# Down products of three feed-forward stages with act stationary and turned back to features

## The chip, the cores and the metric

The kernel runs on one core of a Trainium2 chip. The metric is the device time of one execution in microseconds (us). Five engines work side by side, each through its own queue of instructions: TensorE (PE, with weight loads as PEld), VectorE (DVE), ScalarE (ACT), GpSimd (POOL) and SyncE (SP, which here only issues transfers). They wait for one another by semaphores.

## The reference, cut to what matters

A trunk of two layers on 256 tokens with D = 1024 and a hidden width of 2816. Each layer is a half-weight feed-forward step, a mixer, and another half-weight feed-forward step:

```python
def swiglu(h, w_gate, w_up, w_down):
    return (jax.nn.silu(h @ w_gate) * (h @ w_up)) @ w_down
...
    h = x
    for layer in range(DEPTH):
        h = h + FFN_RESIDUAL_WEIGHT * swiglu(rmsnorm(h, ffn1_norm[layer]), ...)   # weight 0.5
        hn = rmsnorm(h, mix_norm[layer])
        if layer < N_A_LAYERS:
            h = h + mixer_a(hn, a_w_qkv[layer], a_w_o[layer], pos)
        else:
            h = h + mixer_b(hn, b_w_q[j], b_w_o[j], shared[0], shared[1], shared[2], pos)
        h = h + FFN_RESIDUAL_WEIGHT * swiglu(rmsnorm(h, ffn2_norm[layer]), ...)
        if layer == N_A_LAYERS - 1:
            shared = shared_kv(h, kv_norm, kv_w, pos)
    return rmsnorm(h, final_norm)
```

Everything is float32. The four feed-forward stages are called f10 (layer 0, first), f20 (layer 0, second), f11 and f21. They stand in the order f10, mixer a, f20, f11, mixer b, f21.

## The kernel before, in words

The residual lives in SBUF as hT: features on the 128 partitions (8 blocks), 256 tokens along the free axis. Norms work on it block by block: Norm.block(k) makes x_n, the block times its gain (ACT the high part, DVE the low part), and adds its square to a running sum ss_n (ACT squares, POOL adds). The column of scales (col_n, a small PE product at L236) is needed only later, as the products run on the unscaled x_n.

A float32 product is made of three products of a rounded type (fp32r): high by high, high by low and low by high. So each weight is split into a high part wh (ACT) and a low part wl (DVE), and so are the activations. There are two forms. With weights stationary (products_t), one matmul moves 512 columns (high and low of 256 tokens, L194) and one moves 256 (L197), and the result has features on the partitions. With activations stationary (product: L183, L185, L187) three matmuls move 512 columns of weights each, and the result has tokens on the partitions.

A feed-forward stage runs over the 22 blocks of 128 of the hidden width, two blocks at a time. ffn_blocks makes gate and up by products_t. close() evacuates a block's two results with joined() (L338: ACT copies one half out of PSUM and DVE adds the other), multiplies by the row of norm scales, takes Silu on ACT, multiplies, and splits the result into high and low: act. Blocks are closed one step behind the products.

The down product has two versions. For f10, f20 and f11, down_t (L319) runs over the eight blocks of features in pairs, each over all 22 hidden blocks, by products_t; when a pair of feature blocks is done, DVE adds both halves into hT (L331) and Norm.block starts the next norm. For f21, down_last (L434) has act stationary. It views the product of each pair of hidden blocks as a 2 by 2 by 2 product of quarters (two halves of tokens, two hidden blocks, two halves of features). Most pairs take eight products; the pairs in FAST (2, 4, 6 and 7) take seven, with sums of quarters on both sides. The sums of activations are made in the gate and up stage (quarter_sums), those of weights in load() by DVE and POOL (L466 to L468, named sum_f_d). The last two pairs (tail) are held, and the four quarters of the result are closed one after another over them. collect() spreads the shared products m1, m5, m6 and m7 over the four quarters.

PSUM has eight banks: five for accumulators (accp, tag acc) and three for turned tiles and others (trp, tag tr). In down_last c11, c12, c21, m1 and m5 are of accp, and c22, m6 and m7 of trp.

The mixers project q, k and v with x_n stationary and run the heads' work from an Agenda: a list of calls with due times in modelled PE microseconds, from which the next call is taken while the projections go on. A pair of heads passes scores, soften (ACT's exponential), scale (L617, by the sums' reciprocals), turn (PE transposes) and values (PE, L636 and L638). The last two pairs of heads have scale on DVE, the others on POOL. The plans written out at the mixer calls give the due times; ending() gives those of the last pairs.

Transfers go mostly through SP's queue in program order; rawp (4 buffers) and wp (8) set how far ahead they run. The opening loads the first gate and up pieces small, two gate pieces and the gains from ACT's queue and the rest, with xT, from SP's.

Of the kernel before, what the change touches and what calls it, by code (L numbers as in the profile page):

```python
# [35 lines left out]
         ("ffn1_norm", 1), ("mix_norm", 1), ("ffn2_norm", 1)]  # L36

# [26 lines left out]
def trunk(ctx: ExitStack, tc: tile.TileContext, a: dict, out: bass.AP):  # L64
# [141 lines left out]
    def by_token(xs):  # L206

        return [[tuple(x[:, i, t * P:(t + 1) * P] for i in range(2)) for x in xs] for t in range(NT)]

    class Norm:  # L210

        def __init__(self, gi, name):
            self.gi, self.name, self.x, self.col, self.row = gi, name, [], None, None
# [103 lines left out]
    def down_t(name, w, blocks, norm):  # L319

        for p in range(KD // 2):
            acs = [acc(f"dn_{name}_{2 * p + b}") for b in range(2)]
            for k0 in range(0, KF, KD):
                k = min(KD, KF - k0)
                ws = unit(f"{name}_{p}_{k0}", k, S, [(None, rows(w, k0, k, p * S, S))])
                cut = [[tuple(v[:, b * P:(b + 1) * P] for v in pair) for pair in ws] for b in range(2)]
                products_t(acs, cut, blocks[k0:k0 + k], k0 == 0, k0 + k == KF)
            for b, ac in enumerate(acs):
                d = 2 * p + b
                for half in (ac[:, :S], ac[:, S:]):  # L330
                    nc.vector.scalar_tensor_tensor(hT[:, d, :], half, 0.5, hT[:, d, :], op0=ALU.mult, op1=ALU.add)  # L331
                norm.block(d)

    def joined(ac, name):

        s = etile(f"j_{name}")
# [524 lines left out]
```

## Time and profile before

| what | value |
|---|---|
| median of 3 runs | 988.2 us (987.77 to 988.45) |
| the profiled execution | 988.49 us, span 986.7 us |
| mean granted TensorE clock | 0.998 |
| busy, share of the span | PE 99%, PEld 86%, DVE 77%, ACT 60%, POOL 20% |
| f10's down (old form) | about 133.1 to 194.3 us |
| f20's down (old form) | about 435.0 to 496.2 us |
| f11's down (old form) | about 619.9 to 681.1 us |
| f21's down (act stationary) | about 923.2 to 980.4 us, then the last norm and the output |

The span runs from the first to the last instruction, and the execution's time has some 1.8 us more around it. A row of the timeline gives start, duration, engine, line, operation, the tile written and those read, and in brackets the idle time before it and what released it. Matmuls are pipelined: what a matmul costs is the time from its start to the next start, not its duration. A row of the windows gives the stretch and its length, then busy time and instructions for PE, PEld, DVE, ACT and POOL, the granted clock, DMA share and GB/s.

### The profile page before, as it was taken

How to read it: one execution, taken by the hardware profiler on the slowest of the kernel's cores; microseconds unless marked ns; L12 is line 12 of the kernel's file. 1: busy time of each engine (PE TensorE's matmuls, PEld its weight loads, DVE VectorE, ACT ScalarE, POOL GpSimd, SP SyncE). 2: the span in 40 equal slices, each digit the busy share in tenths (PEclk: the TensorE clock that was granted, in tenths of full speed). 3: DMA queues.
4: the chain of work that ended last, by engine and by line, in shares of the span. 5: the costliest groups of instructions: out<-in, count | busy, mean ns of one | idle time of the engine just before them, and what ended most of it. 6: DMA issues, size and time to landing. Idle time of an engine off the chain costs nothing.

```text
span 986.7 us, 15270 instructions
## 1 busy us (share of the span) xinstructions
PE 974.5 (99%) x5640; PEld 847.9 (86%) x5640; DVE 755.7 (77%) x1329; ACT 594.3 (60%) x1090; POOL 200.5 (20%) x204
## 2 busy tenths in 40 slices
PE   8999999999999999999999999999999999999997
PEld 5888888888889888888888888888888988888886
DVE  5987866677888788876668887657677878888996
ACT  7656654457776565655546656644577766666562
POOL 3211111122302211110112111011042122112461
PEclk9999999999999999999999999999999999999999
DMA  9786565654433566556655565665544255565341
GB/s 303 244 261 199 175 204 191 213 171 163 134 107 124 171 200 191 184 193 201 201 183 171 176 208 175 201 193 200 191 132 147 90 168 160 183 198 186 129 171 43
DMA packets 152395, 176.03 MB, mean 178 GB/s; under 512 B 3584, under 2 KB 140288, under 8 KB 152320
## 3 DMA queue, kind: packets, MB, share of 16 engines
q1 hardware_dynamic: 151600, 174.24, 55.0%
q8 instruction: 44, 0.72, 0.3%
q10 hardware_dynamic: 720, 0.82, 0.2%
q14 instruction: 31, 0.25, 0.1%
HBM read 173.99 MB, written 1.05 MB: 177 GB/s over the span
## 4 chain that ended last, share of the span: by engine, by line
PE 68%; DVE 2%; ACT 2%; issue 1%; POOL 0%; POOLq 0%; ACTq 0%; DVEq 0%
PE f_g L194 12%; PE f_u L194 12%; PE dn_f L194 8%; PE f_u L197 6%; PE f_g L197 6%; PE dn_f L197 4%; PE dn_f_d L187 1%; PE dn_f_d L185 1%; PE dn_f_d L183 1%; PE q_b L183 1%; PE kv_b L183 1%; PE q_b L187 1%; PE q_b L185 1%; PE kv_b L187 1%; PE kv_b L185 1%
## 5 line engine op out<-in xcount | busy, mean ns | idle before, releaser
L194 PE MATMUL f_g<-x_n,wh_f_g 128*128 128x512 f32 x688 | 180.5, 394 | 0.0
L194 PE MATMUL f_u<-x_n,wh_f_u 128*128 128x512 f32 x688 | 177.3, 390 | 0.0
L370 POOL TENSOR_TENSOR j_f_u<-j_f_u,r_n 128x256 f32<-128x256 f32 x88 | 81.9, 933 | 373.9 <-DVE j_f_u L338 351.5
L194 PEld LDWEIGHTS f_u<-x_n,wh_f_u 128*128 128x128 f32 x688 | 129.1, 188 | 27.3
L194 PEld LDWEIGHTS f_g<-x_n,wh_f_g 128*128 128x128 f32 x688 | 124.0, 189 | 22.8
L194 PE MATMUL dn_f<-act_f,wh_f 128*128 128x512 f32 x528 | 126.5, 391 | 0.0
L158 DVE TENSOR_TENSOR wl_f_u<-raw_f_u,wh_f_u 128x1024 fp32r<-128x1024 f32 x86 | 118.5, 1381 | 1.5 <-ACT wh_f_u L157 1.4
L194 PEld LDWEIGHTS dn_f<-act_f,wh_f 128*128 128x128 f32 x528 | 96.8, 188 | 18.6
L158 DVE TENSOR_TENSOR wl_f_g<-raw_f_g,wh_f_g 128x1024 fp32r<-128x1024 f32 x86 | 103.4, 1230 | 11.7 <-PE f_g L197 6.9
L158 DVE TENSOR_TENSOR wl_f<-raw_f,wh_f 128x1024 fp32r<-128x1024 f32 x72 | 81.8, 1153 | 35.5 <-ACT wh_f L157 26.7
L197 PE MATMUL f_u<-x_n,wl_f_u 128*128 128x256 f32 x688 | 103.3, 283 | 0.0
L197 PE MATMUL f_g<-x_n,wl_f_g 128*128 128x256 f32 x688 | 102.9, 282 | 0.0
L197 PEld LDWEIGHTS f_g<-x_n,wl_f_g 128*128 128x128 f32 x688 | 96.5, 190 | 6.3
L157 ACT ACTIVATE wh_f<-raw_f 128x1024 fp32r<-128x1024 f32 x72 | 67.3, 978 | 49.4 <-PE dn_f L194 27.1
L157 ACT ACTIVATE wh_f_g<-raw_f_g 128x1024 fp32r<-128x1024 f32 x86 | 89.4, 1048 | 11.3 <-issue 6.0
L157 ACT ACTIVATE wh_f_u<-raw_f_u 128x1024 fp32r<-128x1024 f32 x86 | 86.8, 1047 | 15.2 <-PE f_g L194 10.9
L197 PEld LDWEIGHTS f_u<-x_n,wl_f_u 128*128 128x128 f32 x688 | 91.6, 192 | 0.0
L231 POOL TENSOR_TENSOR ss_n<-ss_n,sq_n 128x256 f32<-128x256 f32 x42 | 41.3, 983 | 245.1 <-ACT sq_n L230 244.2
L368 ACT ACTIVATE j_f_g<-j_f_g 128x256 f32<-128x256 f32 x88 | 36.7, 417 | 68.9 <-DVE j_f_g L367 68.3
L95 ACT ACTIVATE act_f<-j_f_g 128x256 fp32r<-128x256 f32 x80 | 33.2, 417 | 66.2 <-DVE j_f_g L378 65.9
L197 PEld LDWEIGHTS dn_f<-act_f,wl_f 128*128 128x128 f32 x528 | 68.1, 191 | 2.8
L197 PE MATMUL dn_f<-act_f,wl_f 128*128 128x256 f32 x528 | 69.0, 283 | 0.0
(555 smaller groups left out, 1788.7 us busy)
## 6 DMA issues: line engine op xcount, KB each, us to landing
raw_f_g<-in_ffn_w_gate_dram SPq DMA_DIRECT2D x43, 1024.0 KB, 5.4
raw_f_u<-in_ffn_w_up_dram SPq DMA_DIRECT2D x43, 1024.0 KB, 5.4
raw_f<-in_ffn_w_down_dram SPq DMA_DIRECT2D x24, 1024.0 KB, 5.1
raw_f_d<-in_ffn_w_down_dram SPq DMA_DIRECT2D x11, 1024.0 KB, 5.0
raw_f<-in_ffn_w_down_dram SPq DMA_DIRECT2D x12, 768.0 KB, 4.6
raw_qka<-in_a_w_qkv_dram SPq DMA_DIRECT2D x16, 512.0 KB, 4.2
raw_va<-in_a_w_qkv_dram SPq DMA_DIRECT2D x4, 1024.0 KB, 5.2
raw_ao<-in_a_w_o_dram SPq DMA_DIRECT2D x4, 1024.0 KB, 5.0
```

Source lines behind the costliest of these rows:

```text
L95: nc.scalar.activation(hi, src, AF.Copy, scale=scale)
L157: nc.scalar.activation(wh, r, AF.Copy)
L158: nc.vector.tensor_sub(wl, r, wh.bitcast(F32))
L183: nc.tensor.matmul(ac, xh, wh, start=first, stop=False)
L185: nc.tensor.matmul(ac, xh, wl, start=False, stop=False)
L187: nc.tensor.matmul(ac, xl, wh, start=False, stop=last)
L194: nc.tensor.matmul(ac, wh, flat(x), start=first and i == 0, stop=False)
L197: nc.tensor.matmul(ac[:, :S], wl, x[:, 0, :], start=False, stop=last and i == len(ws) - 1)
L231: nc.gpsimd.tensor_tensor(self.ss, self.ss, sq, op=ALU.add)
L368: nc.scalar.activation(g, g, AF.Silu)
L370: nc.gpsimd.tensor_tensor(u, u, norm.row, op=ALU.mult)
```

## The change

down_t goes. The body of down_last becomes quartered(), which makes the four quarters and returns close(), and which both down() (f10, f20, f11) and down_last() (f21) call. down() takes 0.5 of the four quarters into SBUF tiles, turns each half of the features back with PE transposes, four to a tile of 512 columns, and DVE adds each tile into two blocks of hT. The first half of the features is turned within the last closing; the second half is put in norm.late and is turned after the first products of what follows: in ffn_blocks after the first hidden block's first feature, in the mixers from the Agenda at 1.5 and 2.0. f10 and f20 take seven products in four pairs, f11 in three, as the places that hold its sums are fewer there (homes). The order in which the accumulators are taken changes: m1, c11, c21, c12 and c22 are of accp, and m5, m6 and m7 of trp.

At the opening, gains and xT are one tensor, and the third gate piece goes to ACT's queue. In the mixers scale is on POOL for all pairs, and mixer a's plan has the turns of its last pairs later.

```diff
@@ -102,13 +105,11 @@
         return trp.tile([P, 512], F32, tag="tr", name=name)
 
 
-    hT = const.tile([P, KD, S], F32, name="hT")
-
-    gT = const.tile([P, len(GAINS) * KD], F32, name="gT")
-    nc.scalar.dma_start(gT, a["gains"])
-    early = [rawp.tile([P, 2, 1, S], F32, tag="raw", name=f"raw_0_{k}") for k in range(2)]
-    for k, raw in enumerate(early):
-        nc.scalar.dma_start(raw[:, 0, 0], a["ffn1_w_gate"][0][k * P:(k + 1) * P, :S])
+    both = const.tile([P, GX + KD * S], F32, name="gains_hT")
+    gT, hT = both[:, :GX], both[:, GX:].rearrange("p (k s) -> p k s", s=S)
+    early = {k: rawp.tile([P, 2, n, S], F32, tag="raw", name=f"raw_0_{k}") for k, n in OPENING[:3]}
+    for k, n in OPENING[:3]:
+        nc.scalar.dma_start(early[k][:, 0], a["ffn1_w_gate"][0][k * P:(k + n) * P, :S].rearrange("(k p) n -> p k n", p=P))
     BF16 = mybir.dt.bfloat16
     fill = const.tile([P, 512], BF16, name="fill")
     nc.vector.memset(fill, 1.0)
...
-        for k, n in ((0, 1), (1, 1), (2, 2), (4, 2), (6, 2)):
-            raw = early[k] if k < len(early) else rawp.tile([P, 2, n, S], F32, tag="raw", name=f"raw_0_{k}")
+        for k, n in OPENING:
+            raw = early.get(k) or rawp.tile([P, 2, n, S], F32, tag="raw", name=f"raw_0_{k}")
             wh, wl = [wp.tile([P, 2, n, S], F32R, tag=tag, name=f"{tag}_0_{k}") for tag in ("wh", "wl")]
             before(k, n)
-            for i, w in list(enumerate((wg, wu)))[k < len(early):]:
+            for i, w in list(enumerate((wg, wu)))[k in early:]:
                 nc.sync.dma_start(raw[:, i], rows(w, k, n, 0, S))
             nc.scalar.activation(wh, raw, AF.Copy)
...
@@ -315,21 +317,6 @@
             self.split(i + LEAD)
             return self.parts[i]
 
-
-    def down_t(name, w, blocks, norm):
-
-        for p in range(KD // 2):
-            acs = [acc(f"dn_{name}_{2 * p + b}") for b in range(2)]
-            for k0 in range(0, KF, KD):
-                k = min(KD, KF - k0)
-                ws = unit(f"{name}_{p}_{k0}", k, S, [(None, rows(w, k0, k, p * S, S))])
-                cut = [[tuple(v[:, b * P:(b + 1) * P] for v in pair) for pair in ws] for b in range(2)]
-                products_t(acs, cut, blocks[k0:k0 + k], k0 == 0, k0 + k == KF)
-            for b, ac in enumerate(acs):
-                d = 2 * p + b
-                for half in (ac[:, :S], ac[:, S:]):
-                    nc.vector.scalar_tensor_tensor(hT[:, d, :], half, 0.5, hT[:, d, :], op0=ALU.mult, op1=ALU.add)
-                norm.block(d)
 
     def joined(ac, name):
 
...
+                    while norm.late:
+                        norm.late.pop(0)()
                 if first is not None:
                     for k in range(KD - 2, KD):
...
@@ -423,21 +412,38 @@
         close_all()
         return blocks
 
-    def ffn(name, layer, which, norm, after, first=None, beside=()):
+    def left_sums(homes):
+
+        sums = {}
+        for i, home in zip(FAST, homes):
+            if home == "qkh":
+                parts = ap_.tile([P, 2, 512], F32R, tag=home, name=f"left_{i}", bufs=2)
+                sums[i] = (parts[:, 0], parts[:, 1])
+            elif home == "pT":
+                sums[i] = tuple(pp.tile([P, 512], F32R, tag=home, name=f"left_{i}_{j}") for j in range(2))
+            else:
+                sums[i] = tuple(xp.tile([P, 512], F32R, tag=f"{home[:2]}{int(home[2]) + j}", name=f"left_{i}_{j}")
+                                for j in range(2))
+        return sums
+
+    def ffn(name, layer, which, norm, after, first=None, beside=(), homes=("kx4", "kx6", "qkh", "qkh")):
         wg, wu, wd = (a[f"ffn{which}_w_{n}"][layer] for n in ("gate", "up", "down"))
-        blocks = ffn_blocks(name, wg, wu, norm, first, beside)
+        sums = left_sums(homes)
+        blocks = ffn_blocks(name, wg, wu, norm, first, beside, sums)
         if which == 1:
             table(AF.Exp, blocks[-1][:, 0, 0:1].bitcast(F32))
-        down_t(name, wd, blocks, after)
-
-
-    def down_last(name, w, blocks, sums, h, weight, part, after, tail=2):
-
-
-
-
-        c11, c12, c21, m1, m5 = [acc(f"dn_{name}_{n}") for n in ("11", "12", "21", "m1", "m5")]
-        c22, m6, m7 = [trt(f"dn_{name}_{n}") for n in ("22", "m6", "m7")]
+        down(f"{name}_d", wd, blocks, sums, after)
+
+
+    def quartered(name, w, acts, sums, weight, collected, tail=2):
+
+
+
+
+
+        blocks = [[tuple(x[:, i, t * P:(t + 1) * P] for i in range(2)) for x in acts] for t in range(NT)]
+        m1, c11, c21, c12, c22 = [acc(f"dn_{name}_{n}") for n in ("m1", "11", "21", "12", "22")]
+        m5, m6, m7 = [trt(f"dn_{name}_{n}") for n in ("m5", "m6", "m7")]
         begun = set()
 
         def add(n, ac, x, ws, last=False):
...
@@ -483,17 +489,13 @@
                 add(n, ac, left, right, last and len(n) == 1)
 
         def collect():
-
             a, b, c, d = [atile([P, 512], name=f"co_{name}_{n}") for n in "abcd"]
             nc.scalar.activation(a, m1, AF.Copy, scale=weight)
             nc.vector.scalar_tensor_tensor(b, m6, weight, a, op0=ALU.mult, op1=ALU.subtract)
-            nc.gpsimd.tensor_tensor(h[0][0], h[0][0], a, op=ALU.add)
             nc.vector.scalar_tensor_tensor(c, m7, weight, b, op0=ALU.mult, op1=ALU.subtract)
             nc.vector.scalar_tensor_tensor(b, m5, -weight, b, op0=ALU.mult, op1=ALU.add)
-            nc.gpsimd.tensor_tensor(h[0][1], h[0][1], b, op=ALU.add)
             nc.vector.scalar_tensor_tensor(d, m5, -weight, c, op0=ALU.mult, op1=ALU.subtract)
-            nc.vector.tensor_add(h[1][0], h[1][0], c)
-            nc.vector.tensor_add(h[1][1], h[1][1], d)
...
@@ -513,18 +515,63 @@
                             add(*quarters[t][c], blocks[t][2 * i + k], ws[2 * k + c])
             else:
                 held += [(2 * i + k, ws[2 * k:2 * k + 2]) for k in range(2)]
-        end = acc(f"dn_{name}_end")[:, :S]
+
+        def close(t, c, cols=slice(0, 512), ac=None, between=None):
+            n = quarters[t][c][0] if ac is None else "end"
+            whole = quarters[t][c][1] if ac is None else ac
+            to = whole[:, :cols.stop - cols.start]
+            for j, (k, ws) in enumerate(held):
+                add(n, to, blocks[t][k], tuple(v[:, cols] for v in ws[c]), k == KF - 1)
+                if between is not None and j == len(held) - 2:
+                    between()
+            return whole
+
+        return close
+
+    def down(name, w, acts, sums, norm):
+
+        outs = []
+        close = quartered(name, w, acts, sums, 0.5, outs.extend)
+
+        def turn(c, half):
+            tr = trt(f"dt_{name}_{c}_{half}")
+            for i in range(2):
+                for t in range(NT):
+                    at = i * S + t * P
+                    nc.tensor.transpose(tr[:, at:at + P], outs[t][c][:, (2 * half + i) * P:(2 * half + i + 1) * P], ident)
+            d = 4 * c + 2 * half
+            h = hT[:, d:d + 2, :]
+            nc.vector.tensor_add(h, tr.rearrange("p (k s) -> p k s", s=S), h)
+            for i in range(2):
+                norm.block(d + i)
+
+        def turn_first():
+            for half in range(2):
+                turn(0, half)
+
+        for c in range(2):
+            for t in range(NT):
+                ac = close(t, c, between=turn_first if (t, c) == (0, 1) else None)
+                nc.vector.scalar_tensor_tensor(outs[t][c], ac, 0.5, outs[t][c], op0=ALU.mult, op1=ALU.add)
+        norm.late += [lambda half=half: turn(1, half) for half in range(2)]
+
+    def down_last(name, w, acts, sums, h, weight, part, after):
+
+
+        def collected(shared):
+            for t in range(NT):
+                for c in range(2):
+                    (nc.vector if t else nc.gpsimd).tensor_tensor(h[t][c], h[t][c], shared[t][c], op=ALU.add)
+
+        close = quartered(name, w, acts, sums, weight, collected)
         for t in range(NT):
             for c in range(2):
-                n, ac = quarters[t][c]
-                cut = 512 if (t, c) != (1, 1) else S
-                for k, ws in held:
-                    add(n, ac[:, :cut], blocks[t][k], tuple(v[:, :cut] for v in ws[c]), k == KF - 1)
+                n = 512 if (t, c) != (1, 1) else S
...
@@ -603,18 +650,18 @@
                 for t, seg in enumerate(segs):
                     nc.vector.tensor_tensor_reduce(sm[:, seg], ps[i][:, seg], mask[:, seg], scale=-SCALE, scalar=3e38,
                                                    op0=ALU.add, op1=ALU.min, accum_out=nm[:, i, t:t + 1])
-                agenda.after(0.7 + 0.7 * i, soften, sm, nm[:, i], ls[:, i], p >= H // 2 - 2)
-
-        def soften(sm, nm, ls, last):
+                agenda.after(0.7 + 0.7 * i, soften, sm, nm[:, i], ls[:, i])
+
+        def soften(sm, nm, ls):
             for t, seg in enumerate(segs):
                 nc.scalar.activation(sm[:, seg], sm[:, seg], AF.Exp, bias=nm[:, t:t + 1], scale=-1.0,
                                      accum_out=ls[:, t:t + 1])
-            agenda.after(1.3, scale, sm, ls, nc.vector if last else nc.gpsimd)
-
-        def scale(sm, ls, engine):
+            agenda.after(1.3, scale, sm, ls)
+
+        def scale(sm, ls):
             nc.vector.reciprocal(ls, ls)
             for t, seg in enumerate(segs):
-                engine.tensor_scalar(sm[:, seg], sm[:, seg], ls[:, t:t + 1], None, op0=ALU.mult)
+                nc.gpsimd.tensor_scalar(sm[:, seg], sm[:, seg], ls[:, t:t + 1], None, op0=ALU.mult)
 
         def turn(p, i):
             tr = trt(f"pt_{name}{p}_{i}")[:, :3 * P]
...
         agenda = Agenda()
+        for norm in {id(norm): norm for norm, _, _ in segs}.values():
+            for i in range(len(norm.late)):
+                agenda.after(1.5 + 0.5 * i, lambda norm=norm: norm.late.pop(0)())
         scores, turn, values = attention(agenda, lambda g: (qks[g], vss.get(g)), mask, name, blocks)
 
...
           [steps(0, 3.0, 8.0, 11.0, 13.8, 16.5, 19.3), steps(1, 3.0, 8.0, 11.0, 13.8, 16.5, 19.3), steps(2, 4.0, 9.2),
-           steps(3, 2.4, 5.0) + ending(7.6)],
+           steps(3, 2.4, 5.4) + ending(8.4)],
           a["a_w_o"][0], masks[:, 0, :], n2)
     ffn("f20", 0, 2, n2, n3)
     kx = []
-    ffn("f11", 1, 1, n3, n5, beside=[lambda k=k: kx.append(gain(k, 3, "kx", "kx")) for k in range(KD)])
+    ffn("f11", 1, 1, n3, n5, homes=("qkh", "qkh", "pT"), beside=[lambda k=k: kx.append(gain(k, 3, "kx", "kx")) for k in range(KD)])
     xkv, xq = by_token(kx), n5.xs()
     wq, wkv = a["b_w_q"][0], a["kv_w"]
     kv = [(n3, xkv, [("k", wkv, g * n, n, g), ("v", wkv, H * DH + g * n, n, g)]) for g in range(2)]
```

More of the change, by code (lines that the diff above doesn't have):

```diff
@@ L206, in by_token @@
     def by_token(xs):
-        return [[tuple(x[:, i, t * P:(t + 1) * P] for i in range(2)) for x in xs] for t in range(NT)]
+        return [lambda k, t=t: tuple(xs[k][:, i, t * P:(t + 1) * P] for i in range(2)) for t in range(NT)]
     class Norm:
         def __init__(self, gi, name):
-            self.gi, self.name, self.x, self.col, self.row = gi, name, [], None, None
+            self.gi, self.name, self.x, self.late, self.col, self.row = gi, name, [], [], None, None
         def block(self, k):
@@ L523, in down_last @@
                 nc.vector.scalar_tensor_tensor(h[t][c], ac, weight, h[t][c], op0=ALU.mult, op1=ALU.add)
-                part(t, slice(c * 512, c * 512 + cut))
+                part(t, slice(c * 512, c * 512 + n))
             if t:
-                for k, ws in held:
-                    add("end", end, blocks[t][k], tuple(v[:, S:] for v in ws[1]), k == KF - 1)
+                end = close(1, 1, slice(S, 512), acc(f"dn_{name}_end")[:, :S])
                 hc = h[1][1][:, S:]
@@ L737, in first @@
     def first(k, n):
[L738 removed]
+        cols = slice(GX + k * S if k else 0, GX + (k + n) * S)
+        nc.sync.dma_start(both[:, cols], a["gains_xT"][:, cols])
         for i in range(k, k + n):
```

24 lines of the change are left out of this document (10 added, 14 removed).

## The prediction

> **What bounds the kernel now.** I read the page first (share of each engine, the slices, the groups), then the windows of the stages that change, then PE's timeline at the seams.
>
> ```profile
> span 986.7 us, 15270 instructions
> PE 974.5 (99%) x5640; PEld 847.9 (86%) x5640; DVE 755.7 (77%) x1329; ACT 594.3 (60%) x1090; POOL 200.5 (20%) x204
> PEclk9999999999999999999999999999999999999999
> ...
> L194 PE MATMUL dn_f<-act_f,wh_f 128*128 128x512 f32 x528 | 126.5, 391 | 0.0
> ...
> L197 PE MATMUL dn_f<-act_f,wl_f 128*128 128x256 f32 x528 | 69.0, 283 | 0.0
> ```
> ```profile
> core 0: us, PE busy (x) PEld busy (x) DVE busy (x) ACT busy (x) POOL busy (x), PEclk, DMA share, GB/s
> 133.10:194.30 61.20, 61.20 (x354) 54.06 (x353) 38.49 (x49) 29.78 (x42) 7.78 (x6) 1.00 0.62 201
> 923.20:981.00 57.80, 57.47 (x266) 47.88 (x264) 50.54 (x54) 28.61 (x42) 28.82 (x14) 1.00 0.29 101
> 800.00:923.00 123.00, 123.00 (x717) 108.76 (x716) 101.33 (x173) 75.20 (x140) 24.58 (x26) 1.00 0.59 188
> ```
>
> PE is busy 99% of the span and the granted clock stands at its top all the way, so the time is the sum of matmul slots plus a few microseconds in which PE waits. The first window is a down of the old form (f10's): gapless, 61.2 us. The second is f21's, which already has act stationary. The third is a gate and up stage that already makes quarter sums (f21's): PE 123.00 of 123 with DVE at 101.33. So fewer matmul slots become time one for one unless a wait takes their place. The profiled run took 988.49 us, of which the span is 986.7; the median shown is 988.2, 0.3 less. I sum against 988.49 and take 0.3 off. A change under 0.2% (2 us) cannot be told from none here.
>
> **The downs of f10, f20 and f11, slots.**
>
> ```profile
> 923.21 0.40 PE L183 MATMUL dn_f_d<-wh_f_d_0a,act_f 128*128 128x512 f32 x1
> 925.28 0.39 PE L183 MATMUL dn_f_d<-wh_f_d_0a,act_f 128*128 128x512 f32 x1
> ...
> 965.17 0.39 PE L187 MATMUL dn_f_d<-wh_f_d_8a,act_f 128*128 128x512 f32 x1
> ```
> ```profile
> 832.81 0.60 PE L789 MATMUL h<-ident,hT 128*128 128x128 f32 x4
> 833.16 2.09 PE L194 MATMUL f_g<-x_n,wh_f_g 128*128 128x512 f32 x8
> ...
> 844.39 0.60 PE L789 MATMUL h<-ident,hT 128*128 128x128 f32 x4
> ```
>
> Removed in each down: 176 matmuls of 512 and 176 of 256 columns (8 feature blocks by 22), 61.2 us by the first window. Added: an ordinary pair of blocks is 8 products of 3 matmuls, a fast one 7, so 7 x 24 + 4 x 21 = 252 matmuls of 512 for f10 and f20, and 8 x 24 + 3 x 21 = 255 for f11. The matmul at 965.17 starts 176 matmuls after that at 925.28, 39.89 us, hence 0.2266 us each; 252 are 57.1 us and 255 are 57.8 us. Turning back adds 16 transposes. The nearest rows are turn_h's: between its groups of four at 832.81 and 844.39 lie 32 pairs of (512, 256); at 61.2/176 = 0.3477 these take 11.13 of the 11.58 us, so four transposes cost 0.45 us and sixteen 1.8. Gain: 61.2 - 57.1 - 1.8 = 2.3 us for f10 and f20 each, 61.2 - 57.8 - 1.8 = 1.6 for f11; together **-6.2 us**.
>
> [...]
>
> **A bank that comes free late.** In quartered() the five accumulators of accp are now m1, c11, c21, c12, c22; before, c22 lay in a bank of trp. The pool's five banks pass on from the last gate and up results, and c22 gets that of the gate of block 21. c22 is begun by the tenth matmul of the down (three each for c11, c12, c21 first); in f21's down of before that is the row at 925.28. It now waits until DVE's joined() has added up that gate. Before, m1 had that bank, and m1 is not used until pair 2. The rows of f21's down start of before, DVE first and POOL below:
>
> ```profile
> 923.07 1.12 DVE L91 TENSOR_TENSOR act_f<-j_f_g,act_f 128x256 fp32r<-128x256 f32 x1 [0.48 <-ACT act_f L95]
> 924.12 2.32 DVE L454 TENSOR_TENSOR wl_f_d_2a<-raw_f_d,wh_f_d_2a 128x1024 fp32r<-128x1024 f32 x1
> 926.36 0.41 DVE L338 TENSOR_TENSOR j_f_g<-f_g,j_f_g 128x256 f32<-128x256 f32 x1
> ...
> 929.48 0.41 DVE L338 TENSOR_TENSOR j_f_u<-f_u,j_f_u 128x256 f32<-128x256 f32 x1
> ```
> ```profile
> 922.62 1.30 POOL L467 TENSOR_TENSOR sum_f_d_2b<-sum_f_d_2ac,raw_f_d 128x512 f32<-128x512 f32 x1 [0.49 <-PE f_u L197]
> 923.87 1.48 POOL L467 TENSOR_TENSOR sum_f_d_4b<-sum_f_d_4ac,raw_f_d 128x512 f32<-128x512 f32 x1
> 925.32 2.26 POOL L468 TENSOR_TENSOR sum_f_d_2d<-sum_f_d_2b,raw_f_d 128x512 f32<-128x512 f32 x1
> ```
> ```profile
> 133.21 0.42 DVE L338 TENSOR_TENSOR j_f_g<-f_g,j_f_g 128x256 f32<-128x256 f32 x1
> ```
>
> DVE works in order: act's low part, wl of pair 2, then the join, which ends at 926.36 + 0.41 = 926.77, where the tenth matmul is due at 925.28: PE stands 1.5 us, and all products behind it with it. The order of DVE's instructions at this place is the same in the four downs of the changed kernel, as POOL's sums now run in all four: 4 x 1.5 = **+6.0 us** (f21's down had no such wait before, so it pays without a gain). The ends: in f10 of before, where no sums ran, the join started 0.12 us after the down did (133.21 against 133.10) and would have cost nothing; if act's low part comes one POOL sum later, some 1.2 us more. So 0 to 2.7 each; I take the f21 row, as the changed stages are copies of that one. m1 now gets the bank of block 21's up result, free at 929.89, and m1 starts after 48 matmuls, 10.9 us into the down: no wait.
>
> The two DVE operations ahead of the join are stretched: 1.12 where the same work needs 0.4, and 2.32 where a lone 128x1024 one needs 1.22 (a row below). Each ends just as a POOL sum does. [...]
>
> **Mixer ends.**
>
> ```profile
> 276.97 0.55 DVE L617 TENSOR_SCALAR sm_a<-sm_a,ls_a 128x128 f32<-128x128 f32 x2
> 277.78 0.55 DVE L617 TENSOR_SCALAR sm_a<-sm_a,ls_a 128x128 f32<-128x128 f32 x2
> ...
> 280.77 0.56 DVE L617 TENSOR_SCALAR sm_a<-sm_a,ls_a 128x128 f32<-128x128 f32 x2
> 281.58 0.55 DVE L617 TENSOR_SCALAR sm_a<-sm_a,ls_a 128x128 f32<-128x128 f32 x2
> 282.33 1.22 DVE L310 TENSOR_TENSOR wl_ao<-raw_ao,wh_ao 128x1024 fp32r<-128x1024 f32 x1 [0.20 <-ACT wh_ao L308]
> ...
> 770.81 1.45 DVE L617 TENSOR_SCALAR sm_b<-sm_b,ls_b 128x128 f32<-128x128 f32 x6
> 772.36 0.55 DVE L617 TENSOR_SCALAR sm_b<-sm_b,ls_b 128x128 f32<-128x128 f32 x2
> ```
> ```profile
> 284.48 0.36 PE L636 MATMUL po_a<-pT_a,vs_a 128*128 128x256 f32 x1 [1.50 <-DVE vs_a L93]
> ...
> 774.57 0.39 PE L636 MATMUL po_b<-pT_b,vs_b 128*128 128x256 f32 x1 [1.02 <-DVE pT_b L91]
> ```
> ```profile
> 270.63 2.99 POOL L617 TENSOR_SCALAR sm_a<-sm_a,ls_a 128x128 f32<-128x128 f32 x4 [6.31 <-DVE ls_a L615]
> ```
>
> These two waits, 1.50 and 1.02, are PE's only ones of size between the opening and the end. Both end with DVE. DVE loses four times 0.55 = 2.2 us just ahead of the first and 2.0 ahead of the second, more than each wait. The scales go to POOL, 2.99/4 = 0.75 us each, in which a late pair's turn could be held; the plan of mixer a therefore moves its turns later (5.0 to 5.4, 7.6 to 8.4). Between -2.5 and +1 I take **-2.0**, nearer the end that the rows name.
>
> **Opening and seams.**
>
> ```profile
> 10.13 0.50 PE L194 MATMUL f_g<-x_n,wh 128*128 128x512 f32 x1 [0.62 <-ACT wh L172]
> ...
> 14.75 0.39 PE L197 MATMUL f_g<-x_n,wl 128*128 128x256 f32 x1 [0.47 <-DVE wl L173]
> ```
> ```profile
> 198.18 0.41 DVE L331 SCALAR_TENSOR_TENSOR hT<-dn_f,hT 128x256 f32<-128x256 f32 x1
> ```
> ```profile
> 199.59 0.74 POOL L231 TENSOR_TENSOR ss_n<-ss_n,sq_n 128x256 f32<-128x256 f32 x1 [1.61 <-ACT sq_n L230]
> ```
> ```profile
> 202.54 0.50 PE L236 MATMUL col_n<-mean,ss_n 128*128 128x1 f32 x4
> ```
>
> The opening loses one load (the gains join xT) and a gate piece goes from SP's queue to ACT's, where two early pieces stand ahead of it. The two waits shown, 1.1 us, are behind weight pieces: between -1.1 (both go) and +1.1 (the up piece lands later by as much) I take **-0.3**. At the seam to mixer a, features 4 to 7 used to arrive one by one, the last add at 198.18; now they come in two turns that start only after three products of the mixer. The last sum of squares ended at 200.33 and its column product starts at 202.54, 2.2 us of cover, of which I expect about all to go: **+0.3** (0 to 1.1). The seams to f11 and mixer b have the same late turns and no column product as near: nothing, and 0.5 each if their transposes come ahead of the closing addition.
>
> Sum: -6.2 + 6.0 - 2.0 - 0.3 + 0.3 = -2.2 us: 986.3 for a run like the profiled one, **986.0** against the median.
>
> **The rivals.**
>
> The bank comes free in time: DVE gets ahead of POOL, as in the 133.21 row. Then 986.0 - 6.0 = 980.0. For it speaks that half a microsecond earlier at 923.07 lets wl of pair 2 pass; against it that the very stage to be copied shows the contrary. It is also where I go if PE reaches the tenth matmul later than I think. Chance 0.20.
>
> Slower: DVE becomes the bound of the three downs. It is busy 38.49 of 61.2 us in f10's down; with the sums and the split of seven factors f21's took 50.54 of 57.8, and f10, f20 and f11 must also split the next stage's first weights and eight normed blocks. From 57.1 us of work on, PE waits for its low parts: at 59 to 60 us, 2.5 us in each down and 7.5 in all, 993.5. Against it: f21's PE was busy 57.47 of 57.80 with that load. Chance 0.25, with the deeper bank wait (2.7 us each, 990.8) in it, since it has the same cause.
>
> Mixer ends and opening bring nothing: POOL's four scales stand in a row of 3 us and hold the turn instead of DVE. 986.0 + 2.3 = 988.3. [...] Chance 0.12.
>
> **How the numbers follow.** The forecast gets 0.43; its own range is 984 to 988. The range runs from 979 (most of the first rival) to 993 (most of the second). Faster by over 0.2% (under 986.2): 0.23 of the forecast, all 0.20 of the first rival, 0.02 of the third: 0.45. Within 0.2%: 0.18 and 0.08, with 0.01 of the slower rival: 0.27. Slower by over 0.2% (above 990.2): 0.02, 0.24 and 0.02: 0.28.
>
> **What would show it.** Right: PE's groups show act-stationary downs at 0.2266 us a matmul, the tenth of each down with about 1.5 us idle put down to DVE's join of block 21's gate, and no idle before the po matmuls at the mixer ends. Wrong: no idle at the tenth matmul (first rival), idle spread over the downs and put down to DVE's wl (second), or the mixers' waits standing with POOL's scale as releaser (third).

## The result and the profile after

The changed kernel takes 1000.55 us (median of 4 runs, 999.73 to 1002.56) against 988.33 us for the kernel before on the same chip: a ratio of 1.0128, 95% interval 1.0116 to 1.0140. It is 1.3% slower, where 0.2% faster was forecast, and outside the range of 979 to 993. The profiled run took 999.77 us, its span is 998.0.

The page of after, its span, the engines and the chain of work that ended last:

```profile
span 998.0 us, 14866 instructions
PE 972.3 (97%) x5391; PEld 834.3 (84%) x5391; DVE 816.0 (82%) x1383; ACT 614.9 (62%) x1131; POOL 262.2 (26%) x242
...
PE 42%; DVE 16%; ACT 7%; issue 4%; POOL 3%; DMA 1%; POOLq 0%; ACTq 0%; DVEq 0%; SPq 0%
```

The same chain before:

```profile
PE 68%; DVE 2%; ACT 2%; issue 1%; POOL 0%; POOLq 0%; ACTq 0%; DVEq 0%
```

PE has less to do (972.3 us against 974.5) in a span that is 11.3 us longer, and the chain, 68% PE before, now runs through DVE, ACT and POOL as well. The stages, from the start of a stage's first matmul to that of the next, show where (the last column is the first experiment below):

| stage | before | after | old order of accumulators |
|---|---|---|---|
| opening, gate and up of f10 | 133.09 | 132.41 | 132.66 |
| down of f10 | 61.25 | 63.94 | 58.04 |
| mixer a | 117.14 | 119.67 | 119.65 |
| gate and up of f20 | 123.57 | 123.56 | 123.56 |
| down of f20 | 61.25 | 61.26 | 58.08 |
| gate and up of f11 | 123.57 | 124.41 | 124.41 |
| down of f11 | 61.25 | 64.51 | 58.75 |
| mixer b | 116.74 | 117.54 | 117.54 |
| gate and up of f21 | 125.35 | 125.33 | 125.33 |
| down of f21 to the end | 63.49 | 65.37 | 63.68 |

The downs, whose slots alone were to make them 2.5 to 3 us shorter (the late half of the turns falls into the next stage), became as long or longer. PE's timeline has one wait in each, at the tenth matmul, the first of c22:

```profile
134.25 0.39 PE L188 MATMUL dn_f_d<-wh_f_d_0a,act_f 128*128 128x512 f32 x1
138.60 0.50 PE L184 MATMUL dn_f_d<-wh_f_d_0a,act_f 128*128 128x512 f32 x1 [3.96 <-DVE j_f_g L325]
...
444.70 0.50 PE L184 MATMUL dn_f_d<-wh_f_d_0a,act_f 128*128 128x512 f32 x1 [2.88 <-DVE j_f_g L325]
...
631.48 0.79 PE L184 MATMUL dn_f_d<-wh_f_d_0a,act_f 128*128 128x512 f32 x1 [4.00 <-DVE j_f_g L325]
...
936.24 0.50 PE L184 MATMUL dn_f_d<-wh_f_d_0a,act_f 128*128 128x512 f32 x1 [1.38 <-DVE j_f_g L325]
```

The bracket counts from the end of the last matmul. Against a slot of 0.227 us the four cost 4.12, 3.05, 4.16 and 1.54 us, 12.9 in all (the first: 138.60 - 134.25 - 0.23). It is the wait for block 21's gate that was forecast, with f21's of the forecast size and the others at two to three times it. Behind f10's wait the clock falls. Windows of after (the granted clock is the third number from the end):

```profile
134.50:138.60 4.10, 0.14 (x2) 0.01 (x1) 3.62 (x5) 3.06 (x6) 4.10 (x3) 1.00 0.00 0
138.60:140.00 1.40, 1.40 (x5) 1.15 (x6) 1.40 (x2) 0.00 (x0) 0.74 (x1) 0.89 0.00 0
140.00:141.00 1.00, 1.00 (x4) 0.77 (x3) 1.00 (x3) 0.74 (x2) 0.36 (x1) 0.50 0.00 0
141.00:142.00 1.00, 1.00 (x4) 0.81 (x3) 0.70 (x1) 0.62 (x1) 1.00 (x1) 0.50 0.65 106
142.00:143.00 1.00, 1.00 (x3) 0.73 (x3) 0.68 (x2) 0.22 (x1) 0.29 (x1) 0.50 0.90 348
143.00:144.00 1.00, 1.00 (x6) 0.80 (x5) 1.00 (x3) 0.98 (x2) 0.00 (x0) 0.95 0.99 410
...
444.70:446.00 1.30, 1.30 (x6) 1.08 (x7) 1.30 (x2) 0.00 (x0) 0.74 (x1) 1.00 0.00 0
...
631.50:633.00 1.50, 1.50 (x4) 1.21 (x5) 1.50 (x2) 0.00 (x0) 0.72 (x1) 0.50 0.00 0
```

From 139.7 to 143.1 PE has half the clock: the microseconds at 0.50 hold 3 or 4 matmuls, the next one 6 (the counts take in those that overlap an edge). The same follows f11's wait, and nothing of the kind f20's. From the table, f10's down is 63.94 - 58.04 - 4.12 = 1.8 us longer than the wait explains, f11's 64.51 - 58.75 - 4.16 = 1.6.

Why the join is late shows on DVE and POOL at f10's start, and on the same two at f21's:

```profile
133.09 1.50 DVE L365 TENSOR_TENSOR j_f_g<-j_f_g,j_f_u 128x256 f32<-128x256 f32 x1 [0.92 <-POOL j_f_u L357]
135.07 0.93 DVE L94 TENSOR_TENSOR act_f<-j_f_g,act_f 128x256 fp32r<-128x256 f32 x1 [0.48 <-ACT act_f L98]
135.92 2.29 DVE L460 TENSOR_TENSOR wl_f_d_2a<-raw_f_d,wh_f_d_2a 128x1024 fp32r<-128x1024 f32 x1
138.13 0.41 DVE L325 TENSOR_TENSOR j_f_g<-f_g,j_f_g 128x256 f32<-128x256 f32 x1
...
931.55 0.42 DVE L365 TENSOR_TENSOR j_f_g<-j_f_g,j_f_u 128x256 f32<-128x256 f32 x1 [0.92 <-POOL j_f_u L357]
932.46 1.15 DVE L94 TENSOR_TENSOR act_f<-j_f_g,act_f 128x256 fp32r<-128x256 f32 x1 [0.48 <-ACT act_f L98]
933.53 2.32 DVE L460 TENSOR_TENSOR wl_f_d_2a<-raw_f_d,wh_f_d_2a 128x1024 fp32r<-128x1024 f32 x1
935.77 0.41 DVE L325 TENSOR_TENSOR j_f_g<-f_g,j_f_g 128x256 f32<-128x256 f32 x1
```
```profile
132.32 0.74 POOL L357 TENSOR_TENSOR j_f_u<-j_f_u,r_n 128x256 f32<-128x256 f32 x1 [5.29 <-DVE j_f_u L325]
133.02 1.28 POOL L473 TENSOR_TENSOR sum_f_d_2b<-sum_f_d_2ac,raw_f_d 128x512 f32<-128x512 f32 x1
134.27 1.45 POOL L473 TENSOR_TENSOR sum_f_d_4b<-sum_f_d_4ac,raw_f_d 128x512 f32<-128x512 f32 x1
135.68 1.45 POOL L474 TENSOR_TENSOR sum_f_d_2d<-sum_f_d_2b,raw_f_d 128x512 f32<-128x512 f32 x1
...
930.77 0.74 POOL L357 TENSOR_TENSOR j_f_u<-j_f_u,r_n 128x256 f32<-128x256 f32 x1 [5.30 <-DVE j_f_u L325]
932.03 1.30 POOL L473 TENSOR_TENSOR sum_f_d_2b<-sum_f_d_2ac,raw_f_d 128x512 f32<-128x512 f32 x1 [0.52 <-PE f_u L198]
```

In f21's down, POOL has multiplied block 20's up result by 931.51, 1.1 us ahead of the down's first matmul (932.63), and must then wait 0.52 for PE before its first sum; DVE's product slips in between and takes 0.42. In f10's down POOL is done at 133.06, 0.65 after the down's start (132.41). Its first sum follows at once, stands ahead of the product (1.50), and the next two stand ahead of act's low part and of wl. So three operations of DVE are held up and not two, and all of it starts later against PE: the product at 133.09 is 0.7 us behind the down's first matmul, where f21's at 931.55 is 1.1 ahead of it. The later start is 1.8 us and the longer product 1.1 of the 2.6 by which f10's wait is the longer one (act's low part gives 0.2 back). In f20 the product starts at 439.16, 0.4 us ahead of the down's first matmul, so that its wait lies between the two.

### The profile page after: what moved, and what is told of

Its sections match the earlier page's. It is cut to its first block, busy times and chain, and to the rows that moved or that the text cites. A ratio compares the mean times of both kernels' runs of the same rounds, so it can differ in the third digit from the quotient of the medians.

```text
span 998.0 us, 14866 instructions
## 1 busy us (share of the span) xinstructions
PE 972.3 (97%) x5391; PEld 834.3 (84%) x5391; DVE 816.0 (82%) x1383; ACT 614.9 (62%) x1131; POOL 262.2 (26%) x242
## 3 DMA queue, kind: packets, MB, share of 16 engines
q10 hardware_dynamic: 848, 1.05, 0.3%
HBM read 173.99 MB, written 1.05 MB: 175 GB/s over the span
## 4 chain that ended last, share of the span: by engine, by line
PE 42%; DVE 16%; ACT 7%; issue 4%; POOL 3%; DMA 1%; POOLq 0%; ACTq 0%; DVEq 0%; SPq 0%
PE f_g L195 4%; PE dn_f_d L184 4%; PE f_u L195 4%; PE dn_f_d L188 4%; PE dn_f_d L186 4%; DVE wl_f_u L159 3%; POOL j_f_u L357 3%; PE f_g L198 2%; PE f_u L198 2%; ACT wh_f_u L158 2%; ACT wh_f_g L158 2%; DVE wl_f_g L159 2%; DVE j_f_g L325 2%; DVE j_f_g L354 2%; DVE j_f_u L325 1%
## 5 line engine op out<-in xcount | busy, mean ns | idle before, releaser
L357 POOL TENSOR_TENSOR j_f_u<-j_f_u,r_n 128x256 f32<-128x256 f32 x88 | 92.4, 1052 | 361.0 <-DVE j_f_u L325 338.2
L159 DVE TENSOR_TENSOR wl_f_u<-raw_f_u,wh_f_u 128x1024 fp32r<-128x1024 f32 x86 | 113.1, 1317 | 2.7 <-ACT wh_f_u L158 2.7
L233 POOL TENSOR_TENSOR ss_n<-ss_n,sq_n 128x256 f32<-128x256 f32 x42 | 38.4, 913 | 176.6 <-ACT sq_n L232 174.6
L98 ACT ACTIVATE act_f<-j_f_g 128x256 fp32r<-128x256 f32 x58 | 23.9, 418 | 56.6 <-DVE j_f_g L365 56.6
L365 DVE TENSOR_TENSOR j_f_g<-j_f_g,j_f_u 128x256 f32<-128x256 f32 x58 | 27.9, 487 | 30.2 <-POOL j_f_u L357 30.2
L325 DVE TENSOR_TENSOR j_f_g<-f_g,j_f_g 128x256 f32<-128x256 f32 x88 | 36.7, 417 | 11.9 <-ACT j_f_g L324 11.9
L324 ACT ACTIVATE j_f_u<-f_u 128x256 f32<-128x256 f32 x88 | 33.0, 375 | 15.6 <-PE row_n L250 14.6
L354 DVE TENSOR_TENSOR j_f_g<-j_f_g,r_n 128x256 f32<-128x256 f32 x88 | 41.4, 474 | 0.7
L664 POOL TENSOR_SCALAR sm_b<-sm_b,ls_b 128x128 f32<-128x128 f32 (+1 forms) x32 | 29.4, 937 | 47.1 <-DVE ls_b L662 29.6
L664 POOL TENSOR_SCALAR sm_a<-sm_a,ls_a 128x128 f32<-128x128 f32 (+1 forms) x32 | 27.9, 890 | 52.4 <-DVE ls_a L662 35.1
```

Source lines behind the costliest of these rows:

```text
L159: nc.vector.tensor_sub(wl, r, wh.bitcast(F32))
L233: nc.gpsimd.tensor_tensor(self.ss, self.ss, sq, op=ALU.add)
L325: nc.vector.tensor_add(s, ac[:, :S], s)
L354: nc.vector.tensor_mul(g, g, norm.row)
L357: nc.gpsimd.tensor_tensor(u, u, norm.row, op=ALU.mult)
L664: nc.gpsimd.tensor_scalar(sm[:, seg], sm[:, seg], ls[:, t:t + 1], None, op0=ALU.mult)
```

## The experiments

**The old order of the accumulators.**

```diff
-        m1, c11, c21, c12, c22 = [acc(f"dn_{name}_{n}") for n in ("m1", "11", "21", "12", "22")]
-        m5, m6, m7 = [trt(f"dn_{name}_{n}") for n in ("m5", "m6", "m7")]
+        c11, c12, c21, m1, m5 = [acc(f"dn_{name}_{n}") for n in ("11", "12", "21", "m1", "m5")]
+        c22, m6, m7 = [trt(f"dn_{name}_{n}") for n in ("22", "m6", "m7")]
```

> The changed kernel with the accumulators taken in the old order: c11, c12, c21, m1 and m5 of accp, and c22, m6 and m7 of trp. Theory (the whole loss is c22 waiting for the bank of block 21's gate): the four waits at the tenth matmul of the downs (4.1, 3.1, 4.2 and 1.5 us in the trace of after, 12.9 in all) go, and with them the stretches at half the granted clock behind the two longest (about 3.3 us together): 1000.5 - 16.2 = about 984.3. Rival (DVE is behind at the start of each down, whatever waits for it): PE waits as long a little later, for m1's bank or a low part of weights, and the time stays within 5 us of after, 995 or more.

983.41 us (983.02 to 984.39), ratio to before 0.9952 (0.9938 to 0.9965). DVE's join is as late as in after, and nobody waits for it. DVE's row and the window of f10's down in this run:

```profile
138.41 0.41 DVE L325 TENSOR_TENSOR j_f_g<-f_g,j_f_g 128x256 f32<-128x256 f32 x1
```
```profile
132.40:190.40 58.00, 58.00 (x263) 48.16 (x262) 50.24 (x56) 33.99 (x49) 26.88 (x11) 1.00 0.62 212
```

PE is busy 58.00 of 58.00 us at full clock with DVE at 50.24. Two lines turn a loss of 12 us into a gain of 5. In none of the four downs does PE wait 0.3 us or more. That DVE would set the pace of the downs is refuted.

**c22 begun later in pair 0.**

```diff
...
+                todo = [(k, t, c) for k in range(2) for t in range(NT) for c in range(2)]
+                if i == 0:
+                    todo.sort(key=lambda x: x[1:] == (1, 1))
...
```

> The changed kernel, in which only the two products of c22 in pair 0 are moved behind the six others of that pair, so that c22 is begun by the nineteenth matmul and not by the tenth. Theory of the bank: PE comes to the bank 9 x 0.227 = 2.0 us later, so each wait is 2.0 us shorter: about 2.1, 1.0, 2.1 and 0; no wait is long enough for the clock to fall: 1000.5 - 7.7 - 3.3 = about 989.5. Rival (DVE sets the pace of the start): the sum of the waits stays, about 1000.

990.56 us (988.89 to 992.51). PE's rows (f21's wait is gone):

```profile
138.76 0.50 PE L184 MATMUL dn_f_d<-wh_f_d_0a,act_f 128*128 128x512 f32 x1 [1.91 <-DVE j_f_g L325]
...
442.81 0.51 PE L184 MATMUL dn_f_d<-wh_f_d_0a,act_f 128*128 128x512 f32 x1 [0.79 <-DVE j_f_g L325]
...
627.44 0.50 PE L184 MATMUL dn_f_d<-wh_f_d_0a,act_f 128*128 128x512 f32 x1 [1.80 <-DVE j_f_g L325]
```

With the slot they are 2.07, 0.95, 1.96 and 0: each of the three long ones is 2 us less to within 0.2, and f21's 1.54 is gone. The part on the clock missed: behind the waits of 2.07 and 1.96 it fell all the same in the profiled run, which took 992.17 (mean granted clock 0.994, against 0.999 in the first experiment); the runs scatter by 3.6 us.

**Fast pairs later.**

```diff
-FAST = (2, 4, 6, 7)
+FAST = (5, 6, 7, 8)
```

> The changed kernel with seven products in the pairs 5, 6, 7 and 8 (f11: 5, 6 and 7) instead of 2, 4, 6 and 7. POOL's sums of weights then come some microseconds into the down, behind the join of block 21's gate. Theory (the join is late since POOL's sums hold up three DVE operations ahead of it in f10, f20 and f11 and two in f21, by 1.1 to 1.3 us each): the join ends 3 to 4 us earlier, and the waits become about 0.7, 0, 0.7 and 0: about 1000.5 - 11.5 - 3.3 = 985.7, if the fast pairs that now follow one another do not make PE wait for low parts. Rival (DVE is late by its own work): the waits stay at 3 to 4 us, 1000.

994.89 us (990.84 to 996.19), a miss: the waits are 2.02, 1.47, 2.07 and 1.41, and behind f10's the clock falls (0.51 from 138 to 141 us). DVE at f10's start:

```profile
132.13 0.42 DVE L94 TENSOR_TENSOR act_f<-j_f_g,act_f 128x256 fp32r<-128x256 f32 x1 [0.48 <-ACT act_f L98]
133.86 1.23 DVE L472 TENSOR_TENSOR sum_f_d_5ac<-raw_f_d 128x1024 f32<-128x1024 f32 x1 [1.31 <-DMA raw_f_d<-in_ffn_w_down_dram]
135.00 1.22 DVE L460 TENSOR_TENSOR wl_f_d_2a<-raw_f_d,wh_f_d_2a 128x1024 fp32r<-128x1024 f32 x1
136.14 0.42 DVE L325 TENSOR_TENSOR j_f_g<-f_g,j_f_g 128x256 f32<-128x256 f32 x1
```

Without POOL's sums the operations are short (0.42 and 1.22), but the edit put a sum ahead of the join in DVE's order that waits 1.31 us for its transfer and takes 1.23. One cause went and another came: it bears on POOL's part without settling it.

**POOL's first sums made by DVE,** behind the join; DVE's order up to there stays that of after.

```diff
+            engine = nc.vector if i in FAST[:2] else nc.gpsimd
-            nc.gpsimd.tensor_tensor(b[:, 0], ac[:, 0], raw[:, 3], op=ALU.add)
+            engine.tensor_tensor(b[:, 0], ac[:, 0], raw[:, 3], op=ALU.add)
...
```

> The changed kernel with POOL's two sums of weights for the first two fast pairs (2 and 4) made by DVE, which does them behind the join of block 21's gate; DVE's order up to that join is as in after. Theory (POOL's sums hold up DVE's operations with two SBUF inputs): the product, act's low part and wl of pair 2 take 0.42, 0.42 and 1.22 us instead of 1.50, 0.93 and 2.29, and the join ends 2.6 us earlier: waits of about 1.4, 0.4, 1.4 and 0 instead of 4.1, 3.1, 4.2 and 1.5, no fall of the clock, about 987.5 in all. Rival (DVE is that slow by itself, or late by its order): the waits stay over 3 us in f10 and f11 and the time over 997.

987.19 us (986.56 to 988.81). DVE, then PE:

```profile
132.66 0.43 DVE L365 TENSOR_TENSOR j_f_g<-j_f_g,j_f_u 128x256 f32<-128x256 f32 x1 [0.91 <-POOL j_f_u L357]
133.57 0.42 DVE L94 TENSOR_TENSOR act_f<-j_f_g,act_f 128x256 fp32r<-128x256 f32 x1 [0.48 <-ACT act_f L98]
133.91 1.22 DVE L460 TENSOR_TENSOR wl_f_d_2a<-raw_f_d,wh_f_d_2a 128x1024 fp32r<-128x1024 f32 x1
135.05 0.42 DVE L325 TENSOR_TENSOR j_f_g<-f_g,j_f_g 128x256 f32<-128x256 f32 x1
```
```profile
135.52 0.50 PE L184 MATMUL dn_f_d<-wh_f_d_0a,act_f 128*128 128x512 f32 x1 [1.31 <-DVE j_f_g L325]
```

The same three operations take 0.43, 0.42 and 1.22 in place of 1.50, 0.93 and 2.29, and the waits are 1.47, 0.34, 1.36 and 0. This settles POOL's part: 2.7 us of each of the three long waits, and all of f21's. The rest of f10's and f11's, 1.4 us, is there without it, with no operation of DVE stretched: what is left is the late closing of block 20 against PE.

**Dummy matmuls in the two longest waits.**

```diff
+                            if (i, k, t, c) == (0, 0, 1, 1) and name in ("f10_d", "f11_d"):
+                                for _ in range(16):
+                                    nc.tensor.matmul(m7, fill[:, :P], fill, start=True, stop=True)
```

> The changed kernel with sixteen dummy matmuls (bf16, 512 columns, into the bank of m7 ahead of its first use) put before the tenth matmul of f10's and f11's downs, where PE waited 4.1 and 4.2 us. They are some 3.5 us of work that nobody needs, within the wait. Theory (an idle PE makes the granted clock fall, and the stretch at half clock behind these two waits is a loss of its own): no stretch at 0.50 behind them, and the time is 3.3 us shorter than that of after although work is added: 997.2. Rival (the clock falls there for another reason): 1000.5 or more.

1000.02 us (998.76 to 1000.64): no gain. Behind f10's wait, of which 0.6 us was left, the clock stayed at 1.00. But it fell behind f20's unfilled wait, 2.98 us here, where in after it had not, and behind f11's, of which 1.9 was left (mean granted clock of the profiled run 0.995). That left the question open, so all four were filled.

**Dummy matmuls in all four waits,** 17, 13, 24 and 7 of them.

> The changed kernel with dummy matmuls (bf16, 512 columns, into the bank of m7 ahead of its first use) before the tenth matmul of all four downs, as many as about fill the waits: 17 for f10, 13 for f20, 24 for f11, 7 for f21. Theory (PE's idle time makes the granted clock fall): no stretch at 0.50 anywhere before the end of the kernel, the waits themselves stay filled, and the time is that of after less 3.3 us: about 997.3, with less scatter from run to run. Rival (the clock falls for another reason): two stretches at 0.50 remain and the time stays at 1000.5 or more.

997.55 us, and the four runs lie within 0.41 us (997.35 to 997.76) where those of after lie within 2.83. Window behind f11's wait:

```profile
630.00:640.00 10.00, 10.00 (x46) 8.04 (x45) 8.70 (x11) 5.27 (x8) 4.59 (x4) 1.00 0.31 105
```

The granted clock is 1.00 in all four downs. 61 matmuls that nobody needs made the kernel 3.0 us faster than after: the fall goes with the idle time. The gain is not the whole price of the two falls, as f11's 24 are too many: c22 starts there at 630.65, 1.0 us after DVE's join has freed its bank.

**The old mixer ends,** on top of the old order of accumulators (the scales of the last two pairs on DVE, mixer a's plan at 5.0 and 7.6).

> The kernel of the first run, with the ends of the mixers as before the change: the last two pairs' scales on DVE, and mixer a's old plan. Theory from the two traces (PE waits 1.66 and 1.19 us at the ends before, 1.78 and 1.13 after): no difference to the first run, within 0.7 us. Rival (the new ends gain 2 us as forecast): 2 us slower than the first run.

984.24 us (984.13 to 985.8), 0.8 more than the first run. The new ends gain under 1 us, not 2, all of it in mixer a (119.65 us in the first run, 120.58 here), where the plan moved too; mixer b, where only the scales moved, takes 117.54 and 117.53. Their waits in after:

```profile
289.97 0.36 PE L683 MATMUL po_a<-pT_a,vs_a 128*128 128x256 f32 x1 [0.79 <-DVE vs_a L96]
...
291.56 0.39 PE L683 MATMUL po_a<-pT_a,vs_a 128*128 128x256 f32 x1 [0.66 <-DVE pT_a L94]
...
783.79 0.39 PE L683 MATMUL po_b<-pT_b,vs_b 128*128 128x256 f32 x1 [0.97 <-DVE pT_b L94]
```

**The last pair's scales on DVE, the pair before on POOL.**

```diff
...
+                agenda.after(0.7 + 0.7 * i, soften, sm, nm[:, i], ls[:, i], p == H // 2 - 1)
...
```

> The kernel of the first run with the scales of only the very last pair of heads on DVE and those of the pair before on POOL. Theory (in the first run the four last scales stand 4.0 us on POOL ahead of the last turn, and DVE has idle time there): the two waits at mixer a's end, 0.93 and 0.82, and that at mixer b's, 1.13, become shorter by 1 us in all: 982.4. Rival (DVE's low parts set the ends, wherever the scales are): no change or up to 0.8 us slower, as with the old ends: 984.2.

983.26 us (983.12 to 983.71): no difference. The waits stay 0.94, 0.75 and 1.15, and still end with DVE's low parts of vs and pT.

**The third gate piece on SP's queue.** (`OPENING[:3]` becomes `OPENING[:2]`, twice.)

> The kernel of the first run with the third gate piece back on SP's queue (gains and xT stay one tensor). Theory from the trace of after, where the first column product came 0.7 us earlier than before: 0.3 to 0.7 us slower than the first run. Rival (the opening is bound by the bytes, in whatever queue): no difference beyond 0.3 us.

983.28 us (983.14 to 983.91): no difference, as the rival had it.

**turn_in of mixer a's first group later.** A new wait of after stands at the seam to mixer a:

```profile
211.88 0.63 PE L741 MATMUL qt_a<-ident,rt_a 128*128 128x128 f32 x4 [1.55 <-ACT wh_qka L310]
```
```profile
210.13 0.69 ACT L752 ACTIVATE rt_a<-qk_a,c_n 128x512 f32<-128x512 f32 x1 [4.58 <-POOL c_n L242]
```

The late turns delay the column of scales; ACT waits 4.58 us for it, and PE 1.7 for rt_a, which ACT evacuates and DVE then rotates until 211.74 (the bracket names an operation of ACT that ran meanwhile). Against the mixer's start the column's product comes 1.6 us later than before (206.16 - 196.35 against 202.54 - 194.34), but the scales 4.1 later: DVE makes v_n behind a weight's low part, and POOL takes 1.63 us for c_n where it took 0.71.

```diff
-                    agenda.after(3.2, turn_in, g, t)
+                    agenda.after(3.2 if i or norm.name != "n1" else 6.0, turn_in, g, t)
...
```

> The kernel with the old order of accumulators (the first run), in which the first group's turn_in in mixer a is due 6.0 after its evacuation and not 3.2. In the first run PE waits 1.75 us there, as the column of scales comes late behind the late turns and ACT's evacuation with it. Theory: PE does four more products first and that wait goes: 983.4 - 1.7 = 981.7. Rival: the later steps of that group move with it, and as much is waited at the mixer's end: 983.4.

981.50 us (981.0 to 981.73), ratio to before 0.9932 (0.9919 to 0.9946): the wait is gone.

**Mixer ends another 0.8 later,** on top of that (ending 9.2 and 11.2).

> The kernel of the run with turn_in later, with the last pairs' turns another 0.8 later in both mixers (ending 9.2 and 11.2). Theory (the last pairs' values come a little before DVE is ready, so PE waits 0.96, 0.83 and 1.13): those waits lose 0.7 us each where other products are left to fill: about 980. Rival (no products are left there): no gain, 981.5, or slower.

980.87 us (980.6 to 981.49), ratio 0.9925 (0.9913 to 0.9937): the fastest, 0.75% faster than before. The gain over the last run is 0.6, not 1.5: at mixer a's end the first wait all but goes and the second grows to the 1.23 below.

```profile
283.64 0.39 PE L683 MATMUL po_a<-pT_a,vs_a 128*128 128x256 f32 x1 [1.23 <-DVE pT_a L94]
```

## Why the prediction was wrong

**The slots of the downs: right.** Forecast -6.2 us. From the table, the downs of the first experiment are 3.21, 3.17 and 2.50 us shorter than before, 8.9 together, and the late halves of the turns come back as 0.84 in f11's gate and up, 0.80 in mixer b and 0.8 in mixer a (eight transposes, from 198.40 to 199.19 in after): -6.4.

**The bank that comes free late: the mechanism right, the size wrong, and this is the step that failed.** Forecast +6.0, four times f21's 1.5; measured 4.12 + 3.05 + 4.16 + 1.54 = 12.9 of waiting and 3.4 of half clock, 16.3 in all, which the first experiment gives back (998.0 to 981.7 in span). Two faults are in it. I took f21's row for all four, "as the changed stages are copies of that one". The instructions are, but not their times against PE: POOL's part in closing block 20 ends 0.65 us after f10's down begins and 1.1 before f21's, so one more of POOL's sums gets ahead (1.1 us), and the chain begins later (1.8 us in f10 and f11, 0.7 in f20). My upper end of 2.7 us allowed for the one sum and not for the late start. Why blocks are closed later in f10 and f11 than in f21 was not tried and stays open. And the trace of before has no idle PE of 2 to 4 us in mid kernel, so that the clock's fall had no row there; I gave it no price.

That POOL's sums hold up DVE's operations is shown by the run in which DVE makes the sums: the three with two SBUF inputs lose their stretch (1.50, 0.93 and 2.29 us become 0.43, 0.42 and 1.22), and the join, which reads one tile from PSUM and one from SBUF, had none (0.41 in f10 of after, within POOL's sum of 137.09 to 139.34, and 0.42 there). They do not end just as a POOL sum does, as the prediction read it: in f21 of before act's low part ends 0.27 and wl 1.09 us behind one, and in f10 of after the three end 0.29, 0.28 and 1.08 behind theirs. One row shows it the other way round: in the run in which DVE makes the sums, POOL's product of 136.88 begins under a sum of DVE (136.65, 0.69 us) and takes 1.05 us, where the one at 131.89, with DVE idle, takes 0.73.

On the clock, the low stretch behind f10's wait goes from 139.68 to 143.09, 3.41 us, and that behind f11's from 631.20 to 634.61, 3.41 as well. The falls of after, these two and the one at 996.43, where PE has run out of work, lie 491.52 and 365.23 us apart, 144 and 107 times 3.413. From these distances I estimate that the clock is set window by window, on a grid of 3.413 us. PE need not be idle all through the window ahead of a fall. Windows of after on this grid, two up to f10's fall and the low one behind it, the two that share f20's wait, and the one ahead of f11's fall:

```profile
132.85:136.27 3.42, 1.79 (x8) 1.13 (x6) 2.70 (x3) 1.65 (x4) 3.42 (x4) 1.00 0.36 143
136.27:139.68 3.41, 1.08 (x5) 0.89 (x6) 3.41 (x3) 1.41 (x3) 3.07 (x2) 1.00 0.00 0
139.68:143.09 3.41, 3.41 (x10) 2.64 (x9) 2.78 (x6) 1.67 (x3) 1.65 (x1) 0.50 0.47 141
...
440.05:443.47 3.42, 1.76 (x8) 1.13 (x6) 2.94 (x3) 2.64 (x6) 3.42 (x4) 1.00 0.02 6
443.47:446.88 3.41, 2.18 (x10) 1.80 (x11) 3.41 (x6) 0.93 (x3) 2.11 (x2) 1.00 0.00 0
...
627.79:631.20 3.41, 0.00 (x0) 0.00 (x0) 3.24 (x3) 2.78 (x6) 3.41 (x3) 1.00 0.01 5
```

PE is busy for 1.08 us of the window ahead of the first fall and for none of the one ahead of the second. An edge of the grid cuts f20's wait in two, which leaves 1.76 and 2.18 us of work, and no fall follows. With f20's wait unfilled in the run that filled f10's and f11's, the cut fell elsewhere: 2.33 of its 2.82 us idle lay in one window, and the clock fell. The traces of all runs bear this out. The clock fell eight times between the opening and the last down, twice each in after and in the runs with c22 later, with the fast pairs later and with two waits filled (mean granted clock 0.994 to 0.996 in these four, 0.998 or 0.999 in the others). Each fall stands behind a window of which PE was busy 0.48 or less (0.32 and 0 in after), and no other window there is under 0.51 (0.515 the lowest in after). That the share of one window decides, and with it the wait's place on the grid, is my estimate from these windows. Two limits remain: no run moved the grid by intent, and at the end, where the last products run out, two windows with 0.46 and 0.48 were not followed by one, so where the limit lies near one half is open.

**Mixer ends:** forecast -2.0, measured -0.8. I read the scales as what made DVE late, but with them gone PE still waits for DVE's low parts of vs and pT. **Opening:** forecast -0.3, no difference measured. **Seam to mixer a:** forecast +0.3 with an end at 1.1; measured 2.0 in the trace (0.25 at the column's product and 1.71 at qt_a), and 1.9 came back when turn_in was moved. I followed the column to PE's product and not further, over DVE and POOL, to ACT's evacuation, which needs it.

**The rivals.** The bank in time gave 980.0; with the old order of accumulators it is 983.4, the difference being the ends and the seam. DVE as the bound (993.5) did not come; its side case, the deeper bank wait at 990.8, was the right mechanism with 10 us too little. With the terms as measured the sum is -6.4 + 16.3 - 0.8 + 0 + 2.0 = 11.1 us, against 11.3 in span. The size of the one wait makes the loss; but with it at the forecast 6.0 the rest as measured still gives +0.8, so the ends and the seam alone would have taken the small gain away.

## What to carry to other kernels

When accumulators are renamed or reordered, follow each PSUM bank to the reader that must free it, and place that reader against the first matmul in the new owner: here two lines were worth 17 us, with all of the arithmetic unchanged. A wait copied from one stage to another must be re-timed against the other stage's own clock of events, the engine's order being the same or not. Here waits of PE of 4.12 and 4.16 us in mid kernel cost their length and then 1.8 and 1.6 us more at half the clock, and with c22 later the clock fell behind waits of 2.07 and 1.96 too.

## What was not expected of the hardware

Of the nine waits of PE of 1.9 us or more in mid kernel, eight were followed by a stretch of 3.41 us at a granted clock of 0.50, which cost 1.6 and 1.8 us where the stages could be compared; waits of 1.75 us and less, the seam's among them, were not. What told them apart in these traces is PE's busy share of one window of the estimated grid, 0.48 or less ahead of each of the eight falls. The clock first rises at another point of the span in each trace: in after matmuls of 512 columns still start 0.43 us apart at 5.84 us, and 0.23 apart at 10.18; in the run with the mixer ends later they start 0.23 apart at 5.49 already. So I take the grid to lie otherwise against the kernel's start in each. The runs lie 2.8 us apart in after (4 runs), 3.6 with c22 later (10) and 0.4 with the waits filled (4). As the kernel before, which has no such waits, spreads over 1.8 us in 15 runs, it is not shown that the falls alone spread the times.
